# FFN weight operands made during the attention and kept in DRAM

## The chip, the cores and the metric

The kernel runs on one core of a Trainium2 chip. The metric is the device time of one execution in microseconds (us). The kernel before takes 3487.3 us, the median of three runs (3483.93 to 3490.97).

## The reference

One block of a transformer on 2048 tokens of 1024 features, float32 throughout: a modulated RMS norm, two mixers side by side (latent attention of 8 heads over 2048 + 256 keys, and a bidirectional retention of 4 heads), an output projection, and a convolutional FFN whose inner width is 2 x 2816. The part that the change touches is the FFN:

```python
def conv_ffn(h, w_up, conv_w, conv_b, w_down):
    u = h @ w_up
    u = lax.conv_general_dilated(u, conv_w[:, None, :], window_strides=(1,), padding=((1, 1),), ...) + conv_b
    a, g = jnp.split(u, 2, axis=-1)
    return (jax.nn.silu(g) * a) @ w_down
...
x_new = x_new + gt2 * conv_ffn(modulate(rmsnorm(x_new, g_norm2[l]), sh2, sc2), w_up[l], conv_w[l], conv_b[l], w_down[l])
x = x_new
return rmsnorm(x, g_final)
```

## The kernel before

Float32 products are made as three matmuls in the type fp32r: an operand is split into a high part (a cast on ScalarE, L67) and a low part (a subtraction, L68, on VectorE or GpSimd), and high x high, high x low and low x high are added in PSUM (`mm3`, L71 to L73, and `prod`, L1151).

The kernel goes through the modulation and the retention's forward pass, the projections of the latent attention, the attention, the output projection and the FFN. The attention (from about 767 to 1720 us) is a loop over 128 steps, 8 heads x 16 tiles of 128 queries. A step makes the scores (L875) in five blocks, moves each out of PSUM with its maximum (VectorE, L877), takes one Exp of 128x2304 (ScalarE, L889), transposes the weights of the step two before (L914) and splits each block into `ph` (ScalarE, L67) and `pl` (VectorE, L68), and multiplies with the values (L929, L930). Four PSUM buffers `tr` hold transposes, three `sc` scores. Beside it the retention's backward pass runs a tile at a time (`ret_back`), with short GpSimd work. Near the end of the attention the output projection's weights are loaded, multiplied with a gate and split.

The FFN (from about 1922 us) works on three chunks of 640, 640 and 768 tokens. In a chunk it goes through 22 pairs of tiles of 128 features, a linear tile A and a gated tile G. The up projection of a pair goes by seven products of half matrices (the scheme of Strassen and Winograd): operands of weights A1, A2, G2, S1 = G1 + G2, S2 = S1 - A1, S3 = A1 - G1, S4 = A2 - S2, with seven operands from the tokens, made once per chunk. `pair` (L1279) makes the seven products of a pair, adds them up on VectorE (L1296), takes the convolution over tokens (`conv`, L1267: one ScalarE and two VectorE instructions for each half), a gate, and the split of the result into `z`. In between stand fills: six matmuls of the down projection for one tile of tokens (`down`, L1345), which VectorE adds into `acc` (L1373) out of two PSUM buffers `d`.

The weights are prepared in each chunk anew. `up_raw` (L1016) loads the two raw tiles of a pair into the slots `ust`; `up_w` (L1040) makes one operand: four sums on VectorE in all (L1048, L1049, L1050, L1053), then a cast on ScalarE and a subtraction on GpSimd for each of seven. It is called by `prep` in `pair`, for the next pair, after the product that frees the buffer. `down` loads half a tile of rows of `w_down`, multiplies it with the gate `gt2` on GpSimd (L1353), and splits it (ScalarE, GpSimd). (These line numbers are of the functions in the profiled kernel.)

A scheduler sets the order of each engine's instructions when the program is built: it lets an instruction pass others of lower rank when it takes it to be ready, and so an engine's queue doesn't stand in the order of the code. On the chip each engine goes through its queue in order. Loads are issued on SyncE's queue (`dma`), stores mostly on ScalarE's (`store`).

Of the kernel before, what the change touches and what calls it, by code (L numbers as in the profile page):

```python
# [18 lines left out]
P = 128  # L19
# [19 lines left out]
def hybrid_block(ctx: ExitStack, tc: tile.TileContext, x, xT, c, cx, c_ctx, w_ada1, b_ada1, w_ada2, b_ada2, g_norm1,  # L39
# [81 lines left out]
    wmx = ExitStack()  # L121
    wmm = wmx.enter_context(tpool(name="wm", bufs=1))
    with ExitStack() as rf:
# [22 lines left out]
        def row_norm(src, xt, pl_, tag):  # L146
            """a token tile and the inverse of its norm"""
# [8 lines left out]
        def prep_norm(ti, pl_, tag):  # L156
            """a token tile with the features on the partitions, and the inverses of the tokens' norms in every partition"""
# [11 lines left out]
        def prep(ti):  # L169
            """normed, modulated and split"""  # L170
# [15 lines left out]
        def kv_state(first, kvs):  # L186
            """states before the first chunk, forward and backward"""
# [22 lines left out]
        # modulation of the first stage and projections of the context, by blocks of 256 features  # L210
        with tpool(name="ada", bufs=1) as ap_, tpool(name="adap", bufs=1, space=PSUM) as pp:
# [8 lines left out]
            # columns: high and low part for c, the same for c_ctx; unsplit beside zeros  # L220
# [32 lines left out]
            def gemv(b, q):  # L253
                """a quarter of the products of c and c_ctx with the weights of a block"""
# [15 lines left out]
            def columns(b):  # L270
                """shift and scale of a block, features on the partitions"""
# [91 lines left out]
        def mod_units(mp):  # L363
            """modulation of the later stages: gt1, sh2, sc2, gt2"""
# [145 lines left out]
    # 4 KB slots, shared by the raw weights of the last stages  # L510
# [37 lines left out]
    with tpool(name="mpw", bufs=1) as wmp, tpool(name="mp", bufs=2) as wk, \  # L548
# [32 lines left out]
        def front(ti):  # L581
            """latents and rotary key of one token tile"""
# [192 lines left out]
    with tpool(name="at", bufs=2) as wk, \  # L775
# [115 lines left out]
        def inv(h, b):  # L891
            """1 / row sums of a block of queries, as a row on 64 partitions"""
# [55 lines left out]

        WO_FILL = [[(j, n) for n in range(n0, n1) for j in range(2)] for n0, n1 in ((0, 1), (1, 4), (4, 8))]
# [595 lines left out]
```

## Time and profile before

| what | value |
|---|---|
| runs, median (lowest to highest) | 3487.3 us (3483.93 to 3490.97) |
| span of the profiled execution | 3483.1 us |
| TensorE (PE) busy | 3301.2 us, 95% |
| weight loads of TensorE (PEld) | 2938.8 us, 84% |
| VectorE (DVE) busy | 2816.8 us, 81% |
| ScalarE (ACT) busy | 1657.4 us, 48% |
| GpSimd (POOL) busy | 1705.5 us, 49% |
| DMA, mean | 113 GB/s |

The page cuts the span into 40 slices of 87 us. VectorE's digits are 8 in the attention and 9 in nearly all slices of the FFN; GpSimd's are 1 and 2 up to slice 20 and 7 to 9 from slice 24 on. The granted clock of TensorE is 9 (90% or more) in every slice. A matmul's busy time overlaps with the next one's, since they are pipelined: its pace is read from the starts of a run of matmuls, not from its duration. The wait lists say which instruction an idle engine waited for.

### The profile page before, as it was taken

Reading aid. Unit: us, or ns where it says so; the run is one execution under the profiler, and the core shown is the slowest. Engines: PE = TensorE matmul, PEld = TensorE weight load, DVE = VectorE, ACT = ScalarE, POOL = GpSimd, SP = SyncE. Lnnn points to the kernel's source line nnn. Section 1 sums busy time; section 2 is a strip of 40 time slices with the busy share of each in tenths; the row PEclk is TensorE's granted clock in tenths of the full one; section 3 lists DMA queues with packets and bytes.
Section 4 is the critical chain, followed back from the end, with each engine's and each line's share of the span. In section 5 each row is a group of like instructions: output and inputs, shape, how many; then the busy total and the mean of one; then the engine's idle time right before and its main releaser. Section 6 shows DMA issues by size and latency. Waiting matters only on the chain. (4 is left out here: it accounts for less than half of the span.)

```text
span 3483.1 us, 53186 instructions
## 1 busy us (share of the span) xinstructions
PE 3301.2 (95%) x19262; PEld 2938.8 (84%) x19262; DVE 2816.8 (81%) x4969; ACT 1657.4 (48%) x2791; POOL 1705.5 (49%) x1440
## 2 busy tenths in 40 slices
PE   7999999999999999999999998998899998899998
PEld 4888889888999999999987887887788887788887
DVE  4666654457888888888765899999999999999998
ACT  4333334336676766776632343444444444333333
POOL 2322223222111111111144899888788887777774
PEclk9999999999999999999999999999999999999999
DMA  7444435773232232221146434223322223321212
GB/s 267 151 154 146 146 111 191 237 248 103 82 95 80 83 89 89 59 77 56 48 145 185 144 119 141 73 73 123 124 80 82 76 73 121 121 67 61 67 61 79
DMA packets 233822, 394.26 MB, mean 113 GB/s; under 512 B 29508, under 2 KB 106948, under 8 KB 233304
## 3 DMA queue, kind: packets, MB, share of 16 engines
q1 hardware_dynamic: 184640, 334.86, 30.3%
q10 hardware_dynamic: 48920, 56.01, 4.8%
q8 instruction: 152, 2.49, 0.3%
q14 instruction: 110, 0.90, 0.1%
HBM read 293.76 MB, written 97.01 MB: 112 GB/s over the span
## 5 line engine op out<-in xcount | busy, mean ns | idle before, releaser
L68 DVE TENSOR_TENSOR pl<-tr,ph 128x512 fp32r<-128x512 f32 (+1 forms) x640 | 389.1, 629 | 85.5 <-ACT ph L67 85.1
L877 DVE TENSOR_SCALAR_CACHE_REDUCE p<-sc 128x512 f32<-128x512 f32 (+1 forms) x640 | 393.0, 628 | 62.2 <-PE sc L875 50.7
L1151 PE MATMUL u<-T,wS 128*128 128x322 f32 (+1 forms) x2376 | 418.3, 323 | 8.2 <-DVE ua L1296 4.7
L67 ACT CAST ph<-tr 128x512 fp32r<-128x512 f32 (+1 forms) x640 | 329.8, 544 | 198.4 <-PE tr L914 190.5
L1151 PEld LDWEIGHTS u<-T,wS 128*128 128x128 f32 x2376 | 392.1, 191 | 27.3 <-issue 5.0
L71 PE MATMUL d<-dw,z 128*128 128x512 f32 x704 | 297.0, 422 | 113.6 <-DVE acc L1373 112.3
L875 PE MATMUL sc<-ka,qp 128*128 128x512 f32 (+1 forms) x1120 | 346.7, 391 | 0.0
L914 PE MATMUL tr<-ident,p 128*128 128x128 f32 x2304 | 343.3, 273 | 0.0
L889 ACT ACTIVATE p<-p,nb 128x2304 f32<-128x2304 f32 x128 | 284.8, 2225 | 64.3 <-DVE nb L884 60.7
L929 PE MATMUL pv<-ph,vv 128*128 128x256 f32 x1152 | 312.5, 297 | 0.0
L914 PEld LDWEIGHTS tr<-ident,p 128*128 128x128 f32 x2304 | 275.7, 140 | 33.8
L930 PE MATMUL pv<-pl,vv 128*128 128x256 f32 x1152 | 292.5, 286 | 0.0
L73 PE MATMUL d<-dw,z 128*128 128x512 f32 x704 | 283.5, 403 | 2.2 <-DVE z L68 2.2
L72 PE MATMUL d<-dw,z 128*128 128x512 f32 x704 | 284.3, 404 | 0.0
L71 PEld LDWEIGHTS d<-dw,z 128*128 128x128 f32 x704 | 135.2, 192 | 160.5 <-DVE acc L1373 139.1
L945 POOL TENSOR_TENSOR oT<-oT,rB 64x512 f32<-64x512 f32 x32 | 41.1, 1285 | 460.3 <-DVE oT L940 455.4
L68 POOL TENSOR_TENSOR wA<-ust,wA 128x512 fp32r<-128x512 f32 x130 | 208.5, 1604 | 82.9 <-ACT wA L67 82.8
L1373 DVE TENSOR_TENSOR acc<-acc,d 128x512 f32<-128x512 f32 x352 | 235.8, 677 | 15.3 <-PE d L73 13.3
L1353 POOL TENSOR_TENSOR dst<-dst,gt 128x512 f32<-128x512 f32 x132 | 237.8, 1815 | 14.4 <-DMA dst<-in_w_down_dram 11.8
L68 POOL TENSOR_TENSOR wS<-ust,wS 128x512 fp32r<-128x512 f32 x130 | 207.3, 1611 | 70.3 <-ACT wS L67 70.3
L68 POOL TENSOR_TENSOR wS<-s,wS 128x512 fp32r<-128x512 f32 x132 | 234.8, 1778 | 7.0 <-ACT wS L67 6.9
L875 PE MATMUL sc<-kp,qp 128*128 128x512 f32 x620 | 232.6, 375 | 0.0
(371 smaller groups left out, 8726.3 us busy)
## 6 DMA issues: line engine op xcount, KB each, us to landing
ust<-in_w_up_dram SPq DMA_DIRECT2D x132, 512.0 KB
dst<-in_w_down_dram SPq DMA_DIRECT2D x132, 256.0 KB
xt<-in_x_dram SPq DMA_DIRECT2D x32, 512.0 KB
wtg<-in_w_ada_dram SPq DMA_DIRECT2D x64, 256.0 KB
qp<-qn_d SPq DMA_DIRECT2D x124, 128.0 KB
v_d<-vt SPq DMA_DIRECT2D x18, 512.0 KB
wt<-in_w_ada_dram SPq DMA_DIRECT2D x16, 512.0 KB
xc<-in_xT_dram SPq DMA_DIRECT2D x16, 512.0 KB
```

Source lines behind the costliest of these rows:

```text
L67: act.copy(hi, src)
L68: (eng or dve).tensor_tensor(out=lo, in0=src, in1=f32(hi), op=ALU.subtract)
L71: pe.matmul(ps, lhsT=l[0], rhs=r[0], start=first, stop=False)
L72: pe.matmul(ps, lhsT=l[0], rhs=r[1], start=False, stop=False)
L73: pe.matmul(ps, lhsT=l[1], rhs=r[0], start=False, stop=last)
L875: pe.matmul(sc[:, 0:cn], lhsT=q[:, a, qs], rhs=(ka if a < 2 else kp)[:, c0:c0 + cn], start=(a == 0), stop=(a == 2))
L877: dve.tensor_scalar(out=p[:, c0:c0 + cn], in0=sc[:, 0:cn], scalar1=SCALE, scalar2=None, op0=ALU.mult, op1=ALU.max, accum_out=mx[:, ci:ci + 1])
L889: act.activation(p, p, AF.Exp, bias=nb, accum_out=state["rs", h, b][:, k:k + 1])
L914: pe.transpose(ps[:, k * P:(k + 1) * P], p[:, (k0 + k) * P:(k0 + k + 1) * P], ident)
L929: pe.matmul(o[:, 0:256], lhsT=vv[:, kk, :], rhs=ph[:, k, :], start=(kk == 0), stop=False)
L930: pe.matmul(o[:, 0:256], lhsT=vv[:, kk, :], rhs=pl[:, k, :], start=False, stop=(kk == NKT - 1))
L1151: pe.matmul(ps[:, 0:nh], lhsT=w[:, a, k, :], rhs=t[b][:, k, :], start=(k == 0 and a == b), stop=(k == HK - 1 and a == 1))
```

## The change

During the attention a generator, `ffn_weights`, makes all operands from the weights once, for the 22 pairs: it loads the raw tiles, makes the sums on GpSimd, splits (cast on ScalarE, subtraction on GpSimd) into a tile `wp`, and stores them into DRAM tensors `upw_d` and `dwn_d`; the tiles of `w_down` are multiplied with `gt2` there too. The store of a tile is issued one operand later than its split. The loop of the attention takes steps of the generator by a formula. In the FFN each operand is a load of 512 KB into one of 11 rotating buffers (five in `uwp`, the two `ust` slots, four in the FFN's pool), issued by `up_load` where the operand of the next pair was made before; `down` loads two ready halves of its weights. The sums, casts, subtractions and products of the weights leave the FFN.

```diff
+    WSET = (("A1", "A2"), ("S3", "G2"), ("S1", "S4"), ("S2",))
+    upw_d = [[dt_([P, len(ks), 2, 512], f"upw_d{f}_{n}", F32R) for n, ks in enumerate(WSET)] for f in range(NF)]
+    dwn_d = [dt_([P, 2, 2, 512], f"dwn_d{f}", F32R) for f in range(NF)]
...
+        def ffn_weights():
+
+            gt2 = slot("th2")
+            dma(gt2, bcast(mod_d[3]))
+            late = []
+
+            def put(dst, src, k):
+                w = wk.tile([P, 2, 2, 512], F32R, name="wp")[:, 0:k]
+                split(w[:, :, 0, :], w[:, :, 1, :], src.rearrange("p (k f) -> p k f", k=k), pool)
+                late.append((dst, w))
+                if len(late) > 1:
+                    dma(*late.pop(0))
+
+            for f in range(NF):
+                ra, rg, s = slot("ust"), slot("ust"), slot("th")
+                dma(ra, w_up[f])
+                dma(rg, w_up[f + NF])
+                h = [slice(0, 512), slice(512, 1024)]
+                yield
+                put(upw_d[f][0], ra, 2)
+                pool.tensor_tensor(out=s[:, h[0]], in0=rg[:, h[0]], in1=rg[:, h[1]], op=ALU.add)
+                yield
+                pool.tensor_tensor(out=rg[:, h[0]], in0=ra[:, h[0]], in1=rg[:, h[0]], op=ALU.subtract)
+                put(upw_d[f][1], rg, 2)
+                yield
+                pool.tensor_tensor(out=ra[:, h[0]], in0=s[:, h[0]], in1=ra[:, h[0]], op=ALU.subtract)
+                pool.tensor_tensor(out=s[:, h[1]], in0=ra[:, h[1]], in1=ra[:, h[0]], op=ALU.subtract)
+                put(upw_d[f][2], s, 2)
+                yield
+                put(upw_d[f][3], ra[:, h[0]], 1)
+                wd = slot("dst")
+                dma(wd, w_down[f * P:(f + 1) * P, :])
+                yield
+                pool.tensor_tensor(out=wd, in0=wd, in1=gt2, op=ALU.mult)
+                put(dwn_d[f], wd, 2)
+                yield
...
+            while prepped < (6 * NF + 1) * (i - 1) // (NI - 18) and prepped <= 6 * NF:
+                next(prep, None)
+                prepped += 1
...
+    USEQ = [(f, k) for _ in CHK for f in range(NF) for k in ("A1", "S1", "S2", "S3", "G2", "A2", "S4")]
+    def up_load(n=1):
+
+        for _ in range(n):
+            m = n_uw[0]
...
+            f, k = USEQ[m]
+            pl_, tag, bufs = UHOME[m % len(UHOME)]
+            w = pl_.tile([P, 2, HK, P], F32R, name=tag, tag=tag, bufs=bufs)
+            n = next(n for n, ks in enumerate(WSET) if k in ks)
+            dma(w.rearrange("p a k f -> p a (k f)"), upw_d[f][n][:, WSET[n].index(k)])
             uw[f, k] = w
...
+        UHOME += [(uwp, f"w{n}", 1) for n in range(5)] + [(raw, "ust", 2)] * 2
...
-            if ti == 10:
-                up_raw(0)
-            if ti >= 11:
-                up_w(0, *(("A1", "S1"), ("S2", "S3"), (), (), ())[ti - 11])
...
+            if ti == 12:
+                up_load(7)
...
+        UHOME += [(w1, f"wx{n}", 1) for n in range(NX)]
+        up_load(NX)
...
-            def prep(*ks):
-                if nxt is not None:
-                    up_w(nxt, *ks)
+            def prep(k):
+                up_load()
...
-                st = wk.tile([P, 512], F32, name="dst", bufs=2)
-                dma(st, w_down[f * P:(f + 1) * P, js])
-                pool.tensor_tensor(out=st, in0=st, in1=gt2[:, js], op=ALU.mult)
-                w = [wk.tile([P, 512], F32R, name=f"dw{a}", bufs=4) for a in range(2)]
-                split(w[0], w[1], st, pool)
-                ws.append(w)
+                w = wk.tile([P, 2, 512], F32R, name="dw", bufs=4)
+                dma(w, dwn_d[f][:, j])
+                ws.append((w[:, 0, :], w[:, 1, :]))
```

How this moves the instructions, at three places. On ScalarE in the middle of the attention, before (`p,rs` is a step's Exp, `ph` the cast of a transposed block, `otmp` a part of the output, `oT_d` and `oR_d` stores):

```order
L889 ACTIVATE p,rs<-p,nb 128x2304
L67 CAST ph<-tr 128x4x128 x2
L67 CAST ph<-tr 128x2x128
L889 ACTIVATE p,rs<-p,nb 128x2304
L61 DMA ri_d<-rt 4x128
L67 CAST ph<-tr 128x4x128 x3
L939 COPY otmp<-pv 64x256
L67 CAST ph<-tr 128x4x128
L67 CAST ph<-tr 128x2x128
L61 DMA oT_d_176<-oT 64x512
```

and with the change (`wp` is a split weight operand on its way to DRAM):

```order
L67 CAST wp<-th 128x2x512
L893 ACTIVATE p,rs<-p,nb 128x2304
L67 CAST wp<-ust 128x512
L61 DMA oT_d_176<-oT 64x512
L67 CAST ph<-tr 128x2x128
L67 CAST ph<-tr 128x4x128 x3
L943 COPY otmp<-pv 64x256
L67 CAST wp<-dst 128x2x512
L67 CAST ph<-tr 128x4x128
L893 ACTIVATE p,rs<-p,nb 128x2304
L67 CAST ph<-tr 128x2x128
L67 CAST wp<-ust 128x2x512
```

Weight casts stand between the casts and Exps of the steps, five for each of 22 tiles; from the first to the last lie 89 Exps.

On GpSimd in the same stage, before (`sb`, `rstd`, `rbB` and `rbA` are of the retention, `oT` of the attention's output):

```order
L802 TENSOR_TENSOR sb<-sb,gch 128x512
L803 TENSOR_TENSOR sb<-sb,rbA 128x512
L87 TENSOR_SCALAR rstd<-bmv 128x4
L88 TENSOR_TENSOR rstd<-rstd,mhalf 128x4
L816 TENSOR_TENSOR rbB<-rbB,rbA 128x512
L804 TENSOR_TENSOR rbA<-rbA,rbB 128x512
L945 TENSOR_TENSOR oT<-oT,rB 64x512
```

and with the change:

```order
L973 TENSOR_TENSOR th<-ust 128x512
L68 TENSOR_TENSOR wp<-ust,wp 128x2x512
L975 TENSOR_TENSOR ust<-ust 128x512
L978 TENSOR_TENSOR ust<-th,ust 128x512
L986 TENSOR_TENSOR dst<-dst,th_7661 128x1024
L979 TENSOR_TENSOR th<-ust 128x512
L68 TENSOR_TENSOR wp<-ust,wp 128x2x512
L68 TENSOR_TENSOR wp<-th,wp 128x2x512
L949 TENSOR_TENSOR oT<-oT,rB 64x512
L806 TENSOR_TENSOR sb<-sb,gch 128x512
L807 TENSOR_TENSOR sb<-sb,rbA 128x512
L68 TENSOR_TENSOR wp<-ust,wp 128x512
```

The instructions that wait for other engines (`oT`, `sb`, `rstd`) now stand among ten instructions per tile of weight work.

On VectorE in a pair of the FFN's second chunk, before (`ust` and `s` are raw weights and their sums):

```order
L1048 TENSOR_TENSOR s_28195<-ust 128x512
L1335 SCALAR_TENSOR_TENSOR th<-th,yg 128x640
L1049 TENSOR_TENSOR ust<-ust 128x512
L1373 TENSOR_TENSOR acc<-acc,d 128x512
L1337 TENSOR_TENSOR th<-th,ya 128x640
L1050 TENSOR_TENSOR ust<-s_28195,ust 128x512
L1296 TENSOR_TENSOR ua<-u_28209,ug 128x322
L1373 TENSOR_TENSOR acc<-acc,d 128x512
L1053 TENSOR_TENSOR s_28338<-ust 128x512
L68 TENSOR_TENSOR z_28243<-th,z_28242 128x640
```

and with the change:

```order
L1356 SCALAR_TENSOR_TENSOR th<-th,yg 128x640
L1389 TENSOR_TENSOR acc<-acc,d 128x512
L1358 TENSOR_TENSOR th<-th,ya 128x640
L1317 TENSOR_TENSOR ua<-u_28536,ug 128x322
L68 TENSOR_TENSOR z_28569<-th,z_28568 128x640
L1389 TENSOR_TENSOR acc<-acc,d 128x512
```

The four sums of the weights are gone, and the rest stands in nearly the same order.

## Rows read from the trace of the kernel before

**Rows 1.** The page's first line.

```profile
span 3483.1 us, 53186 instructions
```

**Rows 2.** Windows: us, busy time of PE, PEld, DVE, ACT, POOL, clock, DMA.

```profile
900.00:1700.00 800.00, 800.00 (x5671) 732.63 (x5670) 672.73 (x1961) 564.51 (x884) 132.53 (x113) 1.00 0.26 76
1922.00:3483.00 1561.00, 1427.96 (x7675) 1296.21 (x7673) 1467.71 (x1594) 640.43 (x1015) 1260.12 (x1040) 0.98 0.28 93
...
600.00:800.00 200.00, 192.12 (x1207) 171.66 (x1206) 105.34 (x258) 81.05 (x169) 47.66 (x57) 0.99 0.75 236
```

**Rows 3.** Waits from 1900 us on: who, for whom, us, times, longest.

```profile
PE d L71 <- DVE acc L1373: 112.3, 87, 5.3
```

**Rows 4.** Groups by form from 1922 us on: busy us, mean ns, idle before.

```profile
L1353 POOL TENSOR_TENSOR dst<-dst,gt 128x512 f32<-128x512 f32 x132 | 237.8, 1815 | 14.4 <-DMA dst<-in_w_down_dram 11.8 <-DVE ya L1273 2.6
...
L68 POOL TENSOR_TENSOR wG<-ust,wG 128x512 fp32r<-128x512 f32 x64 | 103.5, 1617 | 6.0 <-ACT wG L67 6.0
L1053 DVE TENSOR_TENSOR s<-ust 128x512 f32<-128x512 f32 x64 | 103.5, 1618 | 0.7 <-POOL wS L68 0.4
...
L1050 DVE TENSOR_TENSOR ust<-s,ust 128x512 f32<-128x512 f32 x64 | 57.6, 900 | 2.7 <-POOL wA L68 2.6
```

**Rows 5.** Single lines of VectorE: shortest, median, longest ns, first and last start.

```profile
L1053 DVE TENSOR_TENSOR s<-ust x65: 676/1712/3055, 1853.0 to 3414.1; 128x512 f32<-128x512 f32 x65
L1273 DVE SCALAR_TENSOR_TENSOR ya<-ua,cw,ya x66: 877/1910/1996, 1938.4 to 3450.4; 128x644 f32<-128x644 f32 x44, 128x772 f32<-128x772 f32 x22
L1373 DVE TENSOR_TENSOR acc<-acc,d x352: 668/675/691, 1983.3 to 3475.3; 128x512 f32<-128x512 f32 x176
L1296 DVE TENSOR_TENSOR ua<-u,ug x132: 476/485/564, 1933.4 to 3443.6; 128x322 f32<-128x322 f32 x88, 128x386 f32<-128x386 f32 x44
L1337 DVE TENSOR_TENSOR th<-th,ya x66: 809/1293/2983, 1945.7 to 3455.8; 128x640 f32<-128x640 f32 x44, 128x768 f32<-128x768 f32 x22
```

**Rows 6.** Timeline of TensorE, one pair of the second chunk: start, us, instructions.

```profile
2697.31 1.93 PE L1151 MATMUL u<-X,wA 128*128 128x322 f32 x12
...
2707.03 0.50 PE L71 MATMUL d<-dw,z 128*128 128x512 f32 x1 [1.24 <-DVE acc L1373]
...
2713.16 1.95 PE L1151 MATMUL u<-W,wS 128*128 128x322 f32 x12
2714.95 0.41 PE L71 MATMUL d<-dw,z 128*128 128x512 f32 x1
...
2718.38 1.93 PE L1151 MATMUL u<-X,wA 128*128 128x322 f32 x12
```

**Rows 7.** The same in the third chunk: a product, six down matmuls, a product.

```profile
3217.99 2.29 PE L1151 MATMUL u<-V,wA 128*128 128x386 f32 x12
3220.12 0.40 PE L71 MATMUL d<-dw,z 128*128 128x512 f32 x1
...
3221.53 2.29 PE L1151 MATMUL u<-W,wS 128*128 128x386 f32 x12
```

**Rows 8.** TensorE's lines L1151 and L73: ns, first and last start.

```profile
L1151 PE MATMUL u<-X,wA x792: 305/312/442, 1922.4 to 3427.9; 128*128 128x322 f32 x132, 128*128 128x386 f32 x66
...
L73 PE MATMUL d<-dw,z x704: 387/395/632, 1967.9 to 3474.9; 128*128 128x512 f32 x176
```

**Rows 9.** A load of 512 KB and its first user, 1600 to 1610 us.

```profile
L58 SPq DMA_DIRECT2D ust<-in_w_out_dram x1: 351/351/351, 1603.2 to 1603.2; - x1
L522 POOL TENSOR_TENSOR ust<-ust,gtB x1: 2392/2392/2392, 1606.4 to 1606.4; 128x1024 f32<-128x1024 f32 x1
```

**Rows 10.** ScalarE in the attention: the Exp, and a cast of 1024 columns.

```profile
L889 ACT ACTIVATE p<-p,nb x128: 2218/2224/2242, 767.2 to 1719.2; 128x2304 f32<-128x2304 f32 x128
...
L67 ACT CAST wo<-ust x4: 1047/1050/1081, 1598.3 to 1726.5; 128x1024 fp32r<-128x1024 f32 x4
```

**Rows 11.** Groups of GpSimd from 770 to 1900 us, by form.

```profile
L803 POOL TENSOR_TENSOR sb<-sb,rbA 128x512 f32<-128x512 f32 x16 | 20.7, 1292 | 1.2
...
L522 POOL TENSOR_TENSOR ust<-ust,gtB 128x1024 f32<-128x1024 f32 x4 | 9.6, 2405 | 28.6 <-DMA gtB<-mod_d 21.7 <-DMA ust<-in_w_out_dram 6.9
```

More of the change, by code (lines that the diff above doesn't have):

```diff
@@ L947, in pv @@
             store(oT_d[h // 2][row:row + 64, b * QW:(b + 1) * QW], oT)
+        def ffn_weights():
[31 more added lines that the diff above has]
+                yield
+            for dst, w in late:
+                dma(dst, w)
+            yield
         WO_FILL = [[(j, n) for n in range(n0, n1) for j in range(2)] for n0, n1 in ((0, 1), (1, 4), (4, 8))]
@@ L956, in hybrid_block @@
         rets = ret_all()
+        prep = ffn_weights()
+        prepped = 0
         fetch(0)
@@ L1013, in hybrid_block @@
     uw = {}
[L1014 to L1056 removed]
+    USEQ = [(f, k) for _ in CHK for f in range(NF) for k in ("A1", "S1", "S2", "S3", "G2", "A2", "S4")]
+    UHOME = []
+    n_uw = [0]
+    def up_load(n=1):
+        for _ in range(n):
+            m = n_uw[0]
+            if m == len(USEQ):
+                return
+            n_uw[0] += 1
+            f, k = USEQ[m]
[3 more added lines that the diff above has]
+            dma(w.rearrange("p a k f -> p a (k f)"), upw_d[f][n][:, WSET[n].index(k)])
             uw[f, k] = w
@@ L1163, in hybrid_block @@
     COVER = 0
+    NX = 4
     with tpool(name="owp", bufs=1) as wp, tpool(name="ow", bufs=2) as wk, \
@@ L1224, in hybrid_block @@
         uwp = ctx.enter_context(tpool(name="uwp", bufs=1, side="right"))
-        UW = [uwp, None]
+        UHOME += [(uwp, f"w{n}", 1) for n in range(5)] + [(raw, "ust", 2)] * 2
         cw = uwp.tile([P, 2 * NF, 4], F32, name="cw")
@@ L1239, in hybrid_block @@
                 next(tk)
-            if ti == 10:
-                up_raw(0)
-            if ti >= 11:
-                up_w(0, *(("A1", "S1"), ("S2", "S3"), (), (), ())[ti - 11])
-            if ti == 13:
-                up_w(0, "A2", home=(w1, "dst"))
-            if ti == NT - 1:
-                for k, tag in (("G2", "oT0"), ("S4", "oT1")):
-                    up_w(0, k, home=(wk, tag))
+            if ti == 12:
+                up_load(7)
     w0x.close()
@@ L1258, in sx_tile @@
             return sx.tile([P, HK, CNX // 2 + 2], dt, name=f"sx{a}", tag=f"sx{a}")
-        UW[1] = w1
-        up_raw(1)
-        up_raw(2, [wk.tile([P, 512], F32, name="dw0", bufs=4) for _ in range(4)])
-        gt2 = w1.tile([P, D], F32, name="gt2")
-        dma(gt2, bcast(mod_d[3]))
+        UHOME += [(w1, f"wx{n}", 1) for n in range(NX)]
+        up_load(NX)
         junk = w1.tile([P, 512], BF16, name="junk")
@@ L1340, in tail @@
                 zs[f] = z
-            if nxt is not None and (nxt + 1) % NF not in ur:
-                up_raw((nxt + 1) % NF)
             return tail
```

30 lines of the change are left out of this document (removed).

## The prediction

> **What bounds the kernel now.** I read the stages first, from the windows. The profiled execution spans 3483.1 us [rows 1]. In the attention TensorE is busy 800.00 of 800 us, VectorE 84%, ScalarE 71%, GpSimd 17% [rows 2]: TensorE is the bound there and never idle, so nothing done in that stage can gain time, it can only lose some. In the FFN (1922 us to the end) VectorE is busy 1467.71 of 1561 us, GpSimd 1260.12, TensorE less [rows 2]. There TensorE waits, and the waits say for whom: 112.3 us in 87 stops of the down product's first matmul for VectorE's add into `acc`, which frees the PSUM buffer [rows 3]. VectorE is the bound of the FFN, and TensorE comes next.
>
> Two things fill VectorE there. It makes the sums of the weights, four instructions per pair of feature tiles, 63 or 64 of each in the window, from 57.6 to 103.5 us a group [rows 4]. And its other work is stretched: instructions with two operands in SBUF take 1.7 to 1.9 us in the median where the shortest take 0.68 to 0.88 (sum L1053, convolution L1273), while those with an operand in PSUM do not stretch at all (L1373: 668, 675, 691 ns; L1296: 476, 485, 564) [rows 5]. GpSimd is busy 81% of that time [rows 2], and almost all of that is weights: six groups of subtractions and products, the largest 237.8 us, the smallest 103.5 [rows 4].
>
> **What goes from the FFN.** Per pair the change takes away 4 VectorE sums, 7 ScalarE casts and 7 GpSimd subtractions, and per half tile of `w_down` a cast, a product and a subtraction: 264 instructions of VectorE and 594 of ScalarE over the stage, and 726 of GpSimd's. Left on GpSimd are small things. What is left on VectorE per pair, at the shortest durations: 7 adds of 0.49 us, 4 convolution steps of 0.88, 3 others of 0.81, 5 adds into `acc` of 0.675 [rows 5], which is 3.4 + 3.5 + 2.4 + 3.4 = 12.7 us.
>
> TensorE's own pace comes from runs of matmuls without a stop. Twelve matmuls of 322 columns take 1.79 us from start to start (2713.16 to 2714.95) [rows 6], twelve of 386 columns 2.13 us, six of the down product 1.41 us (3217.99 to 3220.12 to 3221.53) [rows 7]. A pair in the first two chunks has 7 products and 5 token tiles of down product: 7 x 1.79 + 5 x 1.41 = 19.6 us; in the third, 7 x 2.13 + 6 x 1.41 = 23.4 us. Now a pair of the second chunk takes 2697.31 to 2718.38, 21.1 us, with a stop of 1.24 us for `acc` among it [rows 6]. With 12.7 us of VectorE against 19.6 us of TensorE the bound passes to TensorE. The stage's work on TensorE is 44 x 19.6 + 22 x 23.4 = 1377 us. It lasts from the first product at 1922.4 us [rows 8] to the end, 1561 us; the last matmul starts at 3474.9 [rows 8], so 8 us are the end's tail, which stays. That leaves 176 us of stops. The 112 us for `acc` go. Of the other 64 (transitions between chunks, where the operands from the tokens are loaded and split, and the start) I keep half, since those splits are not touched but run on freer engines. FFN afterwards: 1377 + 8 + 32 = 1417 us, **144 us less**; all stops gone would be 176, and half of the `acc` stops alone 56.
>
> **What the loads cost.** Per pair 7 loads of 512 KB for the up weights and, on average, 2 for the down weights: 4.7 MB, against 1.6 MB before. The stage at 600 us moved 236 GB/s over 200 us with the DMA engines busy 0.75 [rows 2]; at that rate 4.7 MB take 20.0 us, about TensorE's 19.6, and with the engines full (236 / 0.75 = 315 GB/s, an estimate) 15 us. Eleven buffers stand between a load and its product, so a load is asked for ten products ahead, some 28 us, and a 512 KB load is in use 3.2 us after its issue (1603.2 to 1606.4) [rows 9]. I cost it at nothing; the products hide it. If 236 GB/s were the ceiling it would cost 44 x 0.4 = 18 us. SyncE's queue is in order, so a load that waits for its buffer holds up `dw` and `acc` loads behind it; they have a whole unit of 20 us in hand. The first pair's operands were made during the output projection; what that frees there I count at 0.
>
> **What comes to the attention.** 22 feature tiles, each with five ScalarE casts (four of 1024 columns at 1.05 us [rows 10], one of 512, at most that), and on GpSimd four sums of 512 columns at 1.29 us, a product and four splits of 1024 at 2.40 (one split of 512 besides, about 1.3) [rows 11]: 4.8 to 5.3 us of ScalarE and 18.5 us of GpSimd for one. By the instruction order the 22 tiles lie beside 89 of the 128 softmax steps, not beside the 110 that the loop's formula names. A step is (1719.2 - 767.2) / 127 = 7.50 us [rows 10], so a tile has 89 x 7.50 / 22 = 30.3 us. GpSimd then has 18.5 us and its old 17%, 5 us: 78%. ScalarE goes from 71 to 87%. TensorE is paced by ScalarE's casts and VectorE's subtractions out of the four `tr` buffers; it already rides out the 2.2 us of every Exp [rows 10] without a stop [rows 2], and a weight cast is half as long. All 110 casts uncovered would be 110 x 1.05 = 115 us, all covered 0; a gain is excluded, TensorE has nothing to give back. I take a tenth, **11 us**, nearer to the covered end because of the Exp row. GpSimd's waiting instructions there (`oT` for VectorE, `rstd` for `bmv`) now stand among weight work; behind them wait casts on ScalarE and stores on SyncE. SyncE gets 110 stores of 0.5 or 1 MB, each waiting for a GpSimd split, and 66 loads; behind them stand the `qp`, `ka`, `vv` and `rB` loads. Two `qp` buffers of four steps each leave 30 us for that. The bytes, 132 MB in 667 us, add 198 GB/s to the 76 of now [rows 2]: 274, below the 315 above.
>
> VectorE's main instructions of the attention read PSUM, one of them with one SBUF operand (as L1373, which does not stretch at 81% GpSimd [rows 2, 5]), so I add nothing. The subtraction L68 is of that form; L877, which also writes out a maximum, has no row beside a busy GpSimd. The Trainium skill (SBUF — State Buffer, "Who interferes with whom") says that a VectorE instruction contends with GpSimd if it has two SBUF inputs or runs in a two-port mode, and that the form that also writes its accumulator does not enter that mode. By that rule the term stays 0; the row of L1053 agrees that two SBUF inputs do contend, and if L877 were hit like it, by 1.0 us five times in each of 89 steps, VectorE would need some 11.3 us per step and the attention 340 us more.
>
> **Sum.** Before 3487 (the median; the profiled span is 4 us under it, and the sum carries over). 3487 - 144 + 11 = **3354 us**.
>
> **Rivals.** (a) *The attention is dragged.* ScalarE's order is fixed, and a weight cast that stands ahead of a softmax cast waits for GpSimd's sum, for a load, or for the store two casts back. If a tile needs 33 us instead of 30.3, TensorE follows: 22 x 2.7 = 59 us, 3413. For it: GpSimd at 78%, loads that land 3.2 us late; against: the sum of 23.5 us leaves 7 us. (b) *The FFN does not reach TensorE's pace*, because waits in VectorE's fixed order remain: a gain of 56 to 80 us, about 3430. For it: the transitions; against: 12.7 us beside 19.6. (c) *Slower: loads one at a time.* If each load starts only when the one before has landed (SyncE held at each buffer), a pair takes 9 x 3.2 = 28.8 us and the FFN 66 x 28.8 + 40 = 1941 us, the whole 3878. It turns slower than before from 2.7 us per load on (9 x 2.7 = 24 us, the mean pair of now). Against it: 236 GB/s in [rows 2] are 2.2 us per 512 KB. [...]
>
> **Chances.** Forecast 3354 (3315 to 3390): 0.70. (a) 0.15, (b) 0.09, (c), the drag from 36 us per tile on, or L877 stretched, all slower: 0.04; no change by other ways 0.02. For 8 in 10 the range takes the forecast's cases and the nearer half of (a) and (b): 3310 (stops nearly all gone) to 3425. Within 0.2%, about 7 us, is what a measurement cannot tell from no change. Faster 0.94, same 0.02, slower 0.04.
>
> **What would show it.** Right: in the FFN GpSimd below 20% busy, convolution steps near 0.9 us, VectorE near 60%, the wait for `acc` nearly gone, TensorE above 97%, and a pair at 19.6 and 23.4 us; in the attention TensorE's stops of some 10 us, VectorE's means unchanged. (a) would show as ScalarE idle before `ph` or `wp` casts with GpSimd or a DMA as releaser and steps above 7.6 us; (b) as stops of `d` or `u` for VectorE; (c) as stops of `u` for DMA of `w`. The forecast fails if the softmax steps grow by more than 0.4 us, or if products wait for their weights.

## The result and the profile after

| | before | after |
|---|---|---|
| median of the runs beside each other | 3485.7 us (4 runs, 3483.93 to 3490.97) | 3342.9 us (4 runs, 3339.3 to 3348.7) |
| ratio, 95% interval | | 0.959 (0.9577 to 0.9604) |
| span of the profiled execution | 3483.1 us | 3340.1 us |

The kernel is 143 us faster; forecast were 133 (3354 us, range 3310 to 3425). That the sum is near is luck in part: two misses, of 28 and of 25 us, have opposite signs, and 8.5 us come from a stage that the change does not touch. The stages show it. A stage goes from the first or last TensorE instruction of its kind to the next; the numbers are read from the starts in the traces.

| stage | before | after | change | forecast |
|---|---|---|---|---|
| up to the first score | 762.4 | 753.9 | -8.5 | 0 |
| attention, first score to last product with the values | 973.0 | 1009.2 | +36.2 | +11 |
| output projection, from there to its last matmul | 186.8 | 187.8 | +1.0 | 0 |
| FFN, from there to the end | 1560.9 | 1389.2 | -171.7 | -144 |

No edit touches the first stage. It takes 760.0 to 762.4 us in the three profiles without the preparation, and 753.9 to 760.6 us in those with it; why is open, and its 8.5 us are not read as an effect. One execution of start_later, the profiled one, ran at a granted clock of 0.848 (0.99 in its others) and took 3552 us; below, start_later has the median of its other four, and no stages.

**The FFN.** The windows of after (columns as in [rows 2]), the attention and then the FFN up to its last matmul:

```profile
900.00:1700.00 800.00, 784.26 (x5450) 708.82 (x5449) 660.84 (x1895) 610.58 (x942) 462.62 (x294) 1.00 0.65 217
1951.00:3332.00 1381.00, 1370.24 (x7671) 1277.35 (x7669) 903.53 (x1331) 301.94 (x422) 79.07 (x318) 1.00 0.73 252
```

In the second row TensorE is busy 1370.24 of 1381 us, VectorE 65%, GpSimd 6% (before: 81% [rows 2]). The DMA engines moved 252 GB/s where [rows 2] had 93. The wait that led the list in [rows 3] is nearly gone. The waits of after from 1951 us on (who, for whom, us, times, longest), first of TensorE's that is left, then of VectorE, which now waits for TensorE:

```profile
PE u L1182 <- ACT ug L1319: 5.8, 1, 5.8
...
DVE acc L1389 <- PE d L73: 221.9, 194, 2.8
```

The group of the down product from 1500 us on has 0.7 us of waits for `acc` (112.3 in [rows 3]). A convolution step, whose shortest, median and longest were 877, 1910 and 1996 ns in [rows 5], now stays at its shortest:

```profile
L1295 DVE SCALAR_TENSOR_TENSOR ya<-ua,cw,ya x66: 878/885/1021, 1971.2 to 3308.5; 128x644 f32<-128x644 f32 x44, 128x772 f32<-128x772 f32 x22
```

The pair has TensorE's pace. Two first products in a row in the second chunk, and two in the third (start, us, instruction; [rows 6] has 21.1 us between two):

```profile
2719.55 1.95 PE L1182 MATMUL u<-X,ust 128*128 128x322 f32 x12
2738.96 1.94 PE L1182 MATMUL u<-X,w 128*128 128x322 f32 x12
...
3122.95 2.28 PE L1182 MATMUL u<-X,wx 128*128 128x386 f32 x12
3146.12 2.29 PE L1182 MATMUL u<-X,ust 128*128 128x386 f32 x12
```

That is 19.4 and 23.2 us.

TensorE itself became quicker, too: it is busy 1370.24 us with the products for which [rows 2] have 1427.96. A part of that is its clock. In the FFN before, the granted clock stood at the lower of its two levels (1.2 GHz) in 16 short stretches, 72 us in all, each of them beside a stop of TensorE of 1.9 to 5.3 us; the page's digits of 9 hide them. One of them, as a window of before (columns as in [rows 2]) and as TensorE's timeline:

```profile
2152.20:2155.60 3.40, 3.38 (x9) 2.80 (x10) 3.37 (x5) 1.08 (x3) 3.40 (x4) 0.52 0.01 2
```
```profile
2152.22 0.74 PE L71 MATMUL d<-dw,z 128*128 128x512 f32 x1 [2.59 <-DVE acc L1373]
...
2153.19 0.63 PE L73 MATMUL d<-dw,z 128*128 128x512 f32 x1
2153.62 0.63 PE L71 MATMUL d<-dw,z 128*128 128x512 f32 x1
```

Matmuls of 512 columns start 0.43 us apart there; in [rows 7] six of them take 1.41 us, 0.235 each. After the change two such stretches are left, 14 us. Going by the starts of the matmuls in them, the lower clock cost some 28 us before and 4 after (an estimate).

**The attention.** In the first row above TensorE is idle 15.7 of 800 us, where [rows 2] have none. GpSimd went from 132.53 to 462.62 us and ScalarE from 564.51 to 610.58. The waits of ScalarE's weight casts and of those who wait for ScalarE, 770 to 1750 us:

```profile
POOL wp L68 <- ACT wp L67: 101.0, 40, 12.3
DVE pl L68 <- ACT ph L67: 96.3, 119, 10.9
ACT wp L67 <- DMA upw_d<-wp: 37.7, 23, 12.4
...
PE pv L933 <- ACT ph L67: 11.2, 7, 8.4
...
ACT wp L67 <- DMA dwn_d<-wp: 7.5, 4, 2.9
...
PE tr L918 <- DVE pl L68: 7.3, 8, 2.2
```

ScalarE stands 45 us at weight casts until a store has freed one of the two `wp` buffers, and TensorE and VectorE stand behind its softmax casts. The longest of these, 12.4 us, is the first. The split of that tile is over at 760.3 us, but SyncE reaches its store only at 773.50 (timeline of SyncE):

```profile
763.10 2.47 SPq L58 DMA_DIRECT2D qp<-qn_d  x4
765.98 5.69 SPq L58 DMA_DIRECT2D qp<-qp_d  x4
771.71 0.42 SPq L58 DMA_DIRECT2D rbA<-qb_d  x1
772.17 0.43 SPq L58 DMA_DIRECT2D rbA<-kvb_d  x1
772.65 0.43 SPq L58 DMA_DIRECT2D rbA<-y_d  x1
773.50 0.79 SPq L58 DMA_DIRECT2D upw_d<-wp  x2
```

### The profile page after: what moved, and what is told of

The parts are those of the page before. It is cut to its first block, busy times and chain, and to the rows that moved or that the text cites. A ratio compares the mean times of both kernels' runs of the same rounds, so it can differ in the third digit from the quotient of the medians.

```text
span 3340.1 us, 52561 instructions
## 1 busy us (share of the span) xinstructions
PE 3259.4 (98%) x19262; PEld 2924.3 (88%) x19262; DVE 2261.4 (68%) x4705; ACT 1403.4 (42%) x2307; POOL 917.9 (27%) x934
## 4 chain that ended last, share of the span: by engine, by line
PE 76%; DMA 10%; POOL 5%; DVE 4%; issue 2%; ACT 2%; SPq 1%; ACTq 0%; POOLq 0%; DVEq 0%
PE u L1182 26%; PE sc L879 6%; PE d L73 5%; PE d L72 5%; PE d L71 5%; PE tr L918 4%; PE pj L71 4%; PE pj L73 3%; PE pj L72 3%; DMA upw_d<-wp 3%; PE pv L933 2%; PE pv L934 2%; POOL wp L68 2%; PE op L73 1%; PE op L72 1%
## 5 line engine op out<-in xcount | busy, mean ns | idle before, releaser
L1294 ACT ACTIVATE yg<-ug,cw 128x644 f32<-128x644 f32 (+1 forms) x66 | 63.7, 966 | 687.3 <-DVE ug L1317 687.3
L933 PE MATMUL pv<-ph,vv 128*128 128x256 f32 x1152 | 313.7, 298 | 11.4 <-ACT ph L67 11.2
L73 PE MATMUL d<-dw,z 128*128 128x512 f32 x704 | 277.9, 395 | 2.2 <-DVE z L68 2.2
L71 PE MATMUL d<-dw,z 128*128 128x512 f32 x704 | 276.3, 393 | 0.7 <-DVE acc L1389 0.7
L72 PE MATMUL d<-dw,z 128*128 128x512 f32 x704 | 276.7, 393 | 0.0
L1182 PE MATMUL u<-T,w 128*128 128x322 f32 (+1 forms) x1440 | 249.2, 321 | 2.0 <-ACT T L67 2.0
L1182 PEld LDWEIGHTS u<-T,w 128*128 128x128 f32 x1440 | 235.6, 190 | 11.8 <-ACT T L67 2.4
L933 PEld LDWEIGHTS pv<-ph,vv 128*128 128x128 f32 x1152 | 218.5, 190 | 21.7 <-ACT ph L67 14.9
L934 PEld LDWEIGHTS pv<-pl,vv 128*128 128x128 f32 x1152 | 218.7, 190 | 6.1 <-DVE pl L68 1.9
L71 PE MATMUL pj<-wr,hT 128*128 128x512 f32 x512 | 204.2, 399 | 1.5 <-DVE rt L349 1.5
L72 PE MATMUL pj<-wr,hT 128*128 128x512 f32 x512 | 203.8, 398 | 0.0
```

Source lines behind the costliest of these rows:

```text
L71: pe.matmul(ps, lhsT=l[0], rhs=r[0], start=first, stop=False)
L72: pe.matmul(ps, lhsT=l[0], rhs=r[1], start=False, stop=False)
L73: pe.matmul(ps, lhsT=l[1], rhs=r[0], start=False, stop=last)
L933: pe.matmul(o[:, 0:256], lhsT=vv[:, kk, :], rhs=ph[:, k, :], start=(kk == 0), stop=False)
L934: pe.matmul(o[:, 0:256], lhsT=vv[:, kk, :], rhs=pl[:, k, :], start=False, stop=(kk == NKT - 1))
L1182: pe.matmul(ps[:, 0:nh], lhsT=w[:, a, k, :], rhs=t[b][:, k, :], start=(k == 0 and a == b), stop=(k == HK - 1 and a == 1))
```

## The experiments

Two theories of the attention's 36 us: **S**, the waits for stores that free a `wp` buffer, and **O**, the time that the weight casts take on ScalarE between the softmax casts. A third, **G**, is GpSimd's work, the transfers and the queues, whoever casts. For the FFN: is VectorE's stretch or are its sums what it lost.

The times of all runs; the ratio is to the kernel before, run beside it.

| kernel | us | ratio (95%) | attention | output projection | FFN |
|---|---|---|---|---|---|
| before | 3485.7 | 1 | 973.0 | 186.8 | 1560.9 |
| after | 3342.9 | 0.959 (0.9577 to 0.9604) | 1009.2 | 187.8 | 1389.2 |
| prep_alone | 3520.6 | 1.0106 (1.0088 to 1.0125) | 1011.1 | 186.1 | 1565.5 |
| loads_alone | 3316.0 | 0.9525 (0.9510 to 0.9539) | 981.2 | 188.0 | 1386.4 |
| no_sums | 3358.2 | 0.9645 (0.9631 to 0.9659) | 975.2 | 183.1 | 1439.7 |
| no_gpsimd | 3317.2 | 0.9528 (0.9514 to 0.9542) | 973.1 | 184.8 | 1396.5 |
| prep_nostore | 3510.0 | 1.0073 (1.0058 to 1.0088) | 996.9 | 186.7 | 1565.5 |
| mid_step | 3326.4 | 0.9548 (0.9534 to 0.9563) | 994.0 | 188.3 | 1386.9 |
| half_tiles | 3341.6 | 0.9592 (0.9575 to 0.9609) | 1002.5 | 188.2 | 1389.5 |
| start_later | 3337.6 | 0.9573 (0.9556 to 0.9590) | | | |
| prep_poolcast | 3512.6 | 1.0081 (1.0066 to 1.0096) | 975.5 | 213.0 | 1563.2 |
| best_two | 3337.7 | 0.9581 (0.9565 to 0.9597) | 1001.8 | 187.6 | 1387.2 |
| best_three | 3335.4 | 0.9569 (0.9555 to 0.9584) | 1001.3 | 189.1 | 1385.5 |
| up_only | 3326.5 | 0.9536 (0.9519 to 0.9554) | 978.2 | 189.3 | 1401.6 |

### prep_alone and loads_alone: one half of the change at a time

prep_alone is the kernel before with `ffn_weights` and its calls added; loads_alone is the kernel after with

```diff
-            for f in range(NF):
+            for f in range(1):
...
-            dma(w.rearrange("p a k f -> p a (k f)"), upw_d[f][n][:, WSET[n].index(k)])
+            dma(w.rearrange("p a k f -> p a (k f)"), upw_d[0][n][:, WSET[n].index(k)])
...
-                dma(w, dwn_d[f][:, j])
+                dma(w, dwn_d[0][:, j])
```

> The kernel before, with the preparation and the stores added to its attention and the FFN left as it was (it does not use what is stored). If the stages are independent, the attention loses here what it lost in the changed kernel, 36 us: 3515 to 3522 us, with steps of 7.5 to 8.3 us while the preparation lasts. If the prediction's term is right for the attention by itself and the rest of the 36 us came from the changed FFN's side, 11 us: 3497. If the 8.5 us that the stages ahead of the attention became shorter come with the added buffers in DRAM, the time is 8 us lower than either.

> The changed kernel with the preparation cut to the first of the 22 feature tiles; every load of the FFN takes the operands of that tile, so the loads have the same size and number, and the FFN computes with the wrong weights. If the FFN's gain is its own: an FFN of 1389 us, as in the changed kernel, and an attention of some 973 us, as before: about 3306 us (3300 to 3315). By the prediction's FFN term (144 us): 3341. If a busier attention was part of what the FFN gained (work that had moved ahead of it), above 3315.

Measured: 37.7 us more and 166.9 us less than the 3482.9 us of before beside them. The attention loses its 38 us alone (1011.1 for 973.0), and the FFN gains its 174 alone (1386.4 for 1560.9). In loads_alone the attention is 8 us longer, and all of it lies in the first eight steps, beside the one tile that is prepared. There ScalarE stands 13.75 us before a weight cast until a store has landed. So the stages are independent: one by one the two halves agree with after within 3 us, but for those 8. That first stop is not what after loses, though: its first 16 steps take 118.2 us and those of before 116.8, since before has a stop of 8.1 us of its own there (scores that wait for a buffer `p`). The next 96 steps take 753.8 us for 719.0: 35 of the 36 us arise there. Of their six groups of 16 steps the first five lose 5.6 to 9.4 us each; the last, behind the end of the preparation, loses 0.1.

### no_sums and no_gpsimd: which part freed the FFN

no_sums leaves VectorE's four sums away, and raw blocks stand in for them; no_gpsimd leaves GpSimd's work on the weights away, and the high parts stand in for the low ones (the diff is no_gpsimd's):

```diff
-            split(w[:, 0], w[:, 1], src.rearrange("p (t f) -> p t f", t=HK), pool)
+            act.copy(w[:, 0], src.rearrange("p (t f) -> p t f", t=HK))
...
-                pe.matmul(ps[:, 0:nh], lhsT=w[:, a, k, :], rhs=t[b][:, k, :],
+                pe.matmul(ps[:, 0:nh], lhsT=w[:, 0, k, :], rhs=t[b][:, k, :],
...
-                pool.tensor_tensor(out=st, in0=st, in1=gt2[:, js], op=ALU.mult)
-                w = [wk.tile([P, 512], F32R, name=f"dw{a}", bufs=4) for a in range(2)]
-                split(w[0], w[1], st, pool)
-                ws.append(w)
+                w = wk.tile([P, 512], F32R, name="dw0", bufs=4)
+                act.copy(w, st)
+                ws.append((w, w))
```

> The kernel before without VectorE's four sums per pair (the raw blocks are used in their place, so the weights are wrong); ScalarE's casts and GpSimd's subtractions and products stay. VectorE loses 313 us of its 1468 in the FFN and is left with 17.5 us per pair, GpSimd has 19.1, TensorE 19.6. Theory: VectorE was the one bound, so it falls below TensorE and most of the gain is there already, 130 to 170 us: 3315 to 3355 us. Rival: the weights' way through GpSimd becomes the next bound, since it has as much to do as TensorE and fixed order: 50 to 90 us, 3395 to 3435, with TensorE waiting for GpSimd's subtractions.

> The kernel before without GpSimd's subtractions for the weights and its product for w_down (the high part is used twice, so the low parts are wrong); VectorE's four sums and ScalarE's casts stay. Theory: VectorE's instructions with two operands in SBUF are stretched by GpSimd; convolution steps fall from 1.7 to 0.9 us and sums from 1.2 to 0.7, VectorE has 15.4 us per pair and falls below TensorE's 19.6: 140 to 172 us gained, 3315 to 3347 us. Rival: they are slow by themselves, and only the sums counted: convolution steps stay at 1.7 us and the time within 20 us of the kernel before.

Measured: 124.7 and 165.7 us gained, 3358 us being 3 above the bound that the first theory gave. Windows of the FFN of no_sums and then of no_gpsimd:

```profile
1920.00:3355.00 1435.00, 1388.12 (x7672) 1281.98 (x7670) 1150.75 (x1336) 632.36 (x1015) 1183.92 (x1040) 0.99 0.30 101
...
1918.00:3312.00 1394.00, 1373.16 (x7674) 1273.74 (x7672) 1044.77 (x1594) 643.13 (x1015) 86.85 (x321) 1.00 0.31 104
```

A convolution step (shortest, median, longest) in each of them; the kernel has three more rows of such steps, which no_sums leaves stretched as well (medians 1341 to 1587 ns):

```profile
L1266 DVE SCALAR_TENSOR_TENSOR ya<-ua,cw,ya x66: 878/1910/2062, 1935.8 to 3326.5; 128x644 f32<-128x644 f32 x44, 128x772 f32<-128x772 f32 x22
...
L1273 DVE SCALAR_TENSOR_TENSOR ya<-ua,cw,ya x66: 875/885/1021, 1934.2 to 3282.7; 128x644 f32<-128x644 f32 x44, 128x772 f32<-128x772 f32 x22
```

Without GpSimd's work VectorE keeps all its 1594 instructions, yet is busy 1044.77 us where [rows 2] have 1467.71: the stretch alone was 423 us. Without the sums GpSimd is still busy 83%, the step shown stays at 1910 ns, and 37.0 us of stops for `acc` remain of 112.3. Each of the two edits alone takes VectorE below TensorE, so their gains don't add up: with GpSimd freed nearly the whole gain is there, and the sums might have stayed in the FFN; without the sums nearly three quarters of it are there.

### prep_nostore: the preparation without its stores

prep_alone, with these lines left out:

```diff
-                late.append((dst, w))
-                if len(late) > 1:
-                    dma(*late.pop(0))
```

> The kernel before with the preparation in its attention (loads, casts, sums, splits) but without the 110 stores of its results; the FFN is left as it was and its output is whole. Theory S: the attention loses because ScalarE, in fixed order, waits at a weight cast for the store that frees one of two buffers (41.7 us of such waits where the stores stand); without stores at most a third of the 38 us is left: 3485 to 3495 us, no ScalarE wait for a DMA at these casts. Rival O: it loses because 110 casts (104 us) fill ScalarE; only the one long stop at the first tile (9 us) goes and 25 to 30 us stay: 3508 to 3513 us.

Measured: 26.1 us over before (3510.0 for 3483.9), attention 996.9. That is 12 us less than prep_alone's loss, and 14 in the stage: O's forecast came in and S's did not. As a measure of S it is rough, since more than the stores differs. Without them the scheduler packs the preparation tighter (559 us from the first cast to the last for 710, beside 70 Exps for 89), the engines move 138 GB/s for 275 (windows below), and ScalarE now stands 27.4 us at weight casts for GpSimd, for 15.5 in prep_alone.

### mid_step, half_tiles, start_later: where the casts stand, how the buffers are cut, when it begins

mid_step takes the steps of the generator in the middle of a softmax step, half_tiles gives every operand a buffer and a store of its own, start_later has `max(0, i - 4)` for `(i - 1)` in the loop's formula. The diffs are those of mid_step and half_tiles.

```diff
+            todo_p = max(0, min((6 * NF + 1) * (i - 1) // (NI - 18), 6 * NF + 1) - prepped)
+            todo += [(2.3 + m, lambda *_: next(prep, None), 0, 0) for m in range(todo_p)]
+            prepped += todo_p
...
-            while prepped < (6 * NF + 1) * (i - 1) // (NI - 18) and prepped <= 6 * NF:
-                next(prep, None)
-                prepped += 1
```

```diff
+                for n in range(k):
+                    w = wk.tile([P, 2, 512], F32R, name="wp", bufs=4)
+                    split(w[:, 0, :], w[:, 1, :], src[:, n * 512:(n + 1) * 512], pool)
+                    late.append((dst[:, n], w))
```

> The changed kernel with the weight work of a softmax step called in the middle of the step, ahead of the third or fourth transpose, and not behind its Exp; the same instructions otherwise. Rival O (ScalarE is filled; a cast right behind or ahead of the 2.2 us Exp makes a block of 3.3 us without a softmax cast): 10 to 20 us less than the changed kernel, 3323 to 3333 us. Theory S (waits for stores, wherever the cast stands): within 5 us of 3343.

> The changed kernel with one buffer and one store for each operand (512 KB, four buffers) where two operands shared one (1 MB, two buffers): the memory is the same, the casts are 198 of 0.6 us for 110 of up to 1.05 us (10 us more of ScalarE), and a store is asked for half a put earlier. Theory S: ScalarE's waits for stores fall from 45 us to under 15, and the time by 10 to 20 us, to 3323 to 3333. Rival O: no gain, 0 to 5 us more: 3343 to 3348.

> The changed kernel with the preparation begun three softmax steps later and ended three later, at the same rate. One stop of ScalarE of 12.4 us at the first tile, for a store that shares the queues with the attention's first loads, cost TensorE some 8.4 us. If that is the cause of the slow first eight steps (7.5 us in the mean for 7.1): 6 to 9 us less, 3334 to 3337 us. If any first store stalls so, wherever it stands: 3343, and the stop moves to step 6 or 7.

Measured: mid_step gains 16 us on after (3326.4), the size that O gave. But the edit did not do what O's forecast supposes. The scheduler spreads the casts over the step in either kernel: in the order on ScalarE 27 of mid_step's 110 casts stand right beside an Exp, and 29 of after's; mid_step has them 2.2 softmax casts later in the mean. ScalarE's waits for the stores of `upw_d` have not shrunk either (42.0 us, 29 times; 37.7 in after). So the hit on O's number is luck as far as the Exp goes, and what the 16 us came from was not tested. One thing did shrink: the stretches of more than 4 us between two softmax casts, in the steps 16 to 112, are 8 in mid_step, 17 in after and none in before.

half_tiles gains nothing that the intervals show, and its casts still wait 40.1 us. start_later is 5 us below after, with intervals that overlap. It hardly moves the start: in its order on ScalarE the first two casts still stand ahead of the first Exp, the third comes one step later than in after, and no cast is more than two steps from where after has it. Its premise, that the first stop cost 8.4 us on balance, had been wrong (118.2 us for 116.8, above).

### prep_poolcast: GpSimd casts

prep_alone with

```diff
-                split(w[:, :, 0, :], w[:, :, 1, :], src.rearrange("p (k f) -> p k f", k=k), pool)
+                pool.tensor_copy(w[:, :, 0, :], src.rearrange("p (k f) -> p k f", k=k))
+                pool.tensor_tensor(out=w[:, :, 1, :], in0=src.rearrange("p (k f) -> p k f", k=k), in1=f32(w[:, :, 0, :]), op=ALU.subtract)
```

> The kernel before with the preparation in its attention, as in prep_alone, but with the 110 casts made by GpSimd and none by ScalarE; the stores stay and the FFN is left as it was. Rival O (ScalarE's time, 104 us of casts and its waits at them, is what TensorE loses): the attention's loss of 38 us falls to 12 us or less, 3484 to 3496 us. Rival G (GpSimd's work, the transfers or the queues cost it, whoever casts): 26 us or more stay, 3510 us or more. If GpSimd's casts take as long as its subtractions (2.4 us), it has 28 of 30 us per tile with its old work, the preparation runs late, and stores on SyncE hold up the loads behind them: also above 3510, but with TensorE waiting for DMA.

Measured: 28.1 us over before, which by the time alone speaks for G. The stages say otherwise: the attention takes 975.5 us, 2.5 more than before, and the 26 us stand in the output projection (213.0 for 186.8). The window 900 to 1400 us of prep_alone, prep_nostore, mid_step and prep_poolcast, in this order:

```profile
900.00:1400.00 500.00, 485.10 (x3360) 434.96 (x3359) 409.06 (x1173) 394.04 (x606) 371.94 (x238) 1.00 0.81 275
```
```profile
900.00:1400.00 500.00, 490.75 (x3425) 444.03 (x3424) 418.73 (x1199) 406.64 (x623) 403.37 (x256) 1.00 0.44 138
```
```profile
900.00:1400.00 500.00, 491.93 (x3424) 442.82 (x3424) 420.23 (x1203) 404.16 (x622) 371.89 (x237) 1.00 0.82 281
```
```profile
900.00:1400.00 500.00, 499.55 (x3545) 457.24 (x3544) 430.49 (x1241) 349.71 (x552) 341.74 (x251) 1.00 0.68 229
```

TensorE's idle time is 14.9, 9.3, 8.1 and 0.45 us. With GpSimd still busy 68% and the stores still there (GpSimd now waits for them, 125 us at its casts), nothing of the stops is left: the loss went through ScalarE. ScalarE is not full, 394 of 500 us being busy in prep_alone; what comes late are its softmax casts, for which `pv` waits above. The 26 us come after the attention. The tile's instructions on GpSimd, with first and last start:

```profile
L960 POOL CAST wp<-dst x22: 1033/1041/1052, 807.2 to 1708.4; 128x1024 fp32r<-128x1024 f32 x22
L961 POOL TENSOR_TENSOR wp<-dst,wp x22: 2386/2400/2793, 812.5 to 1716.5; 128x1024 fp32r<-128x1024 f32 x22
```

The preparation's last split now ends at 1719 us, in prep_alone at 1476, and the splits of the output projection's weights queue behind it. The window 1700 to 1760 us, and the first of TensorE's waits there:

```profile
1700.00:1760.00 60.00, 39.76 (x211) 33.13 (x210) 32.02 (x52) 25.90 (x41) 42.70 (x19) 0.82 0.48 162
```
```profile
PE sc L72 <- POOL wo L68: 10.2, 3, 5.1
```

TensorE is idle 20 of 60 us, and the mean of its granted clock falls to 0.82, where the same stretch of before has neither. One thing differs besides the caster: the preparation runs at a lower rate, 960 us from the first cast to the last for 710. A loss in proportion to the rate would still be 28 of the 38 us.

### best_two and best_three: the edits together

best_two is mid_step with start_later's formula; best_three issues each store right behind its split besides (`len(late) > 0`).

> The changed kernel with both edits that took something back: the weight work in the middle of a softmax step, and the preparation begun three steps later. If they are independent: 16 and 5 us, 3322 us (3317 to 3327). If the middle of the step already covers the long stop at the first tile: 3326 as in mid_step.

> The two edits of best_two, and each store asked for right behind its split and not one put later. Theory S: ScalarE's waits for stores, 42 us in mid_step, fall by more than half and 3 to 8 us go: 3312 to 3318 us. Rival: SyncE now stands at each store until GpSimd's split is done (2.4 us and what is queued there), the loads behind it come late: 0 to 10 us more than best_two.

Measured: 3337.7 and 3335.4, 11 and 9 us above mid_step alone; the guess that the edits add up was wrong. For best_two the programs say why: it has the same instructions in the same order on every engine as start_later (3337.6 us), down to the semaphores. With the later formula the scheduler makes nothing of where in the step the calls stand, so best_two is start_later once more, and says nothing on the two edits together. The long first stop is there, too: in best_two ScalarE waits 11.2 us at the weight cast of 788.4 us for a store that SyncE reached at 784.3, and mid_step has it with 10.8 us. It belongs to the first stores, wherever they stand. What makes the attention 7.8 us longer than in mid_step (1001.8 for 994.0) lies behind step 16 (746.2 us for 738.4 up to step 112) and stays open. Issuing the store at once takes the waits from 44.8 to 33.9 us and the time by nothing that the intervals show.

### up_only: GpSimd casts, and w_down stays in the FFN

The kernel after with prep_poolcast's two lines, five generator steps per tile for six, and in `down`

```diff
-                dma(w, dwn_d[f][:, j])
+                st = wk.tile([P, 512], F32, name="dst", bufs=2)
+                dma(st, w_down[f * P:(f + 1) * P, js])
+                pool.tensor_tensor(out=st, in0=st, in1=gt2[:, js], op=ALU.mult)
+                split(w[:, 0, :], w[:, 1, :], st, pool)
```

> The changed kernel with the attention's casts made by GpSimd, as in prep_poolcast, and with w_down left out of the preparation: its product, cast and subtraction stand in the FFN as before the change, one loaded up operand fewer is held ahead there (10 for 11 buffers), and the attention's preparation has 88 puts for 110. If prep_poolcast's 28 us were GpSimd's lateness (its preparation ended 1694 to 1731 us, among the work for the output projection's weights) and nothing else, the preparation now ends before 1600 us, the attention takes 973 to 980 us and the output projection 185; GpSimd is busy some 25 to 30 per cent of the FFN, VectorE has 14 to 16 us per pair for TensorE's 19.6, and the FFN takes 1390 to 1400 us: 3310 to 3330 us, below all kernels before it that compute the whole. Rival: GpSimd is late again: an output projection of 200 us or more, 3335 to 3350. Rival: the stretch of VectorE comes back with GpSimd's 30 per cent: an FFN of 1420 us or more, 3345 and above.

Measured: 3326.5 us, 16 below after, with the stages where they were expected or some 4 us above: attention 978.2, output projection 189.3, FFN 1401.6. Its attention and a stretch of its FFN:

```profile
900.00:1400.00 500.00, 499.90 (x3547) 458.13 (x3546) 426.97 (x1247) 351.67 (x558) 329.39 (x253) 1.00 0.67 223
1950.00:3310.00 1360.00, 1341.21 (x7467) 1247.41 (x7466) 994.85 (x1297) 366.06 (x529) 460.57 (x568) 0.99 0.65 225
```

The attention's loss is down to 5 us, with 88 casts at 9.0 us each for 110 at 6.5. The FFN takes 12 us more than in after, with GpSimd busy 34% and ScalarE's casts back; which of them costs it was not tried. It is, with mid_step, the fastest that computes the whole; both beat the kernel before and the kernel after.

## Why the prediction was right, and where its terms were not

- **The bound.** Right. The attention could only lose and did; the FFN was held by VectorE, and TensorE is its bound now. That the stretch of VectorE came from GpSimd was read from [rows 5]; no_gpsimd shows it.
- **The FFN, -144 for -172.** Mechanism right, the size off by 28 us. The step that failed is "Of the other 64 (transitions between chunks ...) I keep half". TensorE is idle 11 us after, up to the last matmul (1381 - 1370.24), not 32; another 7 us are its own work, 1370 us for the 1377 from single runs of [rows 6, 7]. But the 64 us had not been stops at the transitions. TensorE's idle time before is 1561 - 1427.96 - 8 = 125 us, 112.3 of them for `acc`: all other stops are 13 us, about what is left after. The other 51 are matmuls that take longer than in the runs that the prediction measured; some 28 of these are the lower clock beside the stops, the rest is not resolved. They went with the stops for `acc`, which the prediction had going in full. The tail of 8 us stayed (3331.6 to 3340.1).
- **The loads, 0.** Right: 252 GB/s, above the 236 of [rows 2], and no stop of a product for its weights. Rival (c) is excluded, since a pair would have taken 28.8 us.
- **The attention, +11 for +36.** The step that failed is "I take a tenth, nearer to the covered end because of the Exp row". A third of the 115 us came. That TensorE rides out the Exps as the kernel before places them does not say that it rides out 110 casts more among them; and the term had the casts' own time alone, where ScalarE also stands 45 us at them until a store has landed. Tiles were prepared from 754.4 to 1461.5 us, 32.1 us each, for the 30.3 of the forecast and the 33 of rival (a). So tiles came two thirds of the way to (a), and 25 us of the 59 that (a) adds to the forecast; its sign is there too, ScalarE standing before `wp` casts with a DMA as releaser. That these waits are the larger part of the loss is not shown: 24 of the 38 us stay without the stores (prep_nostore).
- **The bytes.** The prediction's 132 MB are counted in units of 1024 x 1024: the pages have 533.26 MB for prep_alone and 394.26 for before, 139 MB more. It changes nothing in the sum.
- **What the attention's 36 us are.** That they go through ScalarE is shown (prep_poolcast, up_only, both at a lower rate). They arise while the preparation lasts, steps 16 to 96, and the long first stop is hardly among them. What goes along with them is how often ScalarE leaves more than 4 us between two softmax casts. In the steps 16 to 112 there are 17 such stretches in after (35 us lost), 16 in prep_alone (36), 11 in prep_nostore (18), 8 in mid_step (19), 5 in prep_poolcast (2), 4 in up_only (4) and none in before; half_tiles with 9 (28) doesn't fit well. This is read from the traces and not tested by an edit. How much of it is waits for stores (S), and how much the casts' time and place (O), stays open.
- **VectorE's L877.** Right: it has the same 681 to 682 ns for 512 columns from 900 to 1400 us before and in prep_alone, with GpSimd busy 74% in the latter. The Trainium skill (SBUF — State Buffer, "Who interferes with whom") says that this form does not contend and that two inputs in SBUF do; both agree with the traces here, the latter with 885 against 1910 ns.
- **The output projection, 0.** Right (+1.0), as long as the preparation ends ahead of it; prep_poolcast shows the 26 us that it costs otherwise.

## What to carry to other kernels

Where a VectorE-bound stage runs beside a busy GpSimd, take the GpSimd work away first and count VectorE's instructions again at their shortest durations: here that alone was 166 us, without touching VectorE's code. Work that is moved into a stage bound by TensorE is to be put on the engine that does not feed TensorE: GpSimd's casts cost the attention 2.5 and 5 us where ScalarE's cost 21 to 38. What such an engine does late is paid at the next stage's first use, so give the moved work an end and check it there. Where a scheduler sets the order, compare the order that was built before reading an experiment that moves calls: here start_later hardly moved the start, and best_two came out as start_later's program.

## What was not expected of the hardware

- GpSimd casts 128x1024 from f32 to fp32r in 1.04 us, as fast as ScalarE (1.05), though its subtraction of the same size takes 2.40 us. The Trainium skill (GPSIMD Engine Reference, "4.1 Engine selection") says that one input goes at roughly line rate and two at half of VectorE's. Both agree: the cast keeps ScalarE's pace, and 128x512 with two inputs take 1.29 us on GpSimd [rows 11] and 0.68 at the shortest on VectorE [rows 5].
- A convolution step of 128x644 mostly takes either some 0.88 or some 1.95 us; GpSimd's share sets how many are long. Over the four rows of such steps, those above 1.4 us are 1% with GpSimd busy 6% (after), 32% at 34% (up_only), 60% at 83% (no_sums) and 72% at 81% (before), and the means are 894, 1202, 1498 and 1633 ns. A single row's median says little: in up_only the four have 890, 1009, 1010 and 1623 ns.
